# Residual tokens reloaded two at a time into other buffers, and a new order of the mixer's weight rings, in a hybrid decoder layer

## The chip, the core and the metric

The kernel runs on one core of one Trainium2 chip. The metric is device time in microseconds (us), the median of three runs. TensorE (PE) does the matmuls and transposes, VectorE (DVE) and ScalarE (ACT) evacuate and split, GpSimd (POOL) does a few small operations, and SyncE (SP) issues almost all DMAs, in one queue in program order.

## What is computed

One layer on 512 tokens of width 1024, all in float32:

```python
def hybrid_layer(x, ...):
    h = rms_norm(x, ffn1_pre_g)
    x = x + 0.5 * rms_norm(swiglu(h, ffn1_w_gate, ffn1_w_up, ffn1_w_down), ffn1_post_g)
    h = rms_norm(x, mix_pre_g)
    q, k, v, z, xbc, dt = jnp.split(h @ w_in, IN_SPLITS, axis=-1)
    attn = diff_attention(q, k, v, lam, attn_subln_g, lambda_init)
    ssm = ssd_mixer(z, xbc, dt, conv_w, conv_b, dt_bias, a_log, d_skip, ssm_norm_g)
    x = x + rms_norm(jnp.concatenate([attn, ssm], axis=-1) @ w_out, mix_post_g)
    h = rms_norm(x, ffn2_pre_g)
    x = x + 0.5 * rms_norm(swiglu(h, ffn2_w_gate, ffn2_w_up, ffn2_w_down), ffn2_post_g)
    return x
```

The feed-forward width is 2816; the mixer has 8 attention heads with two softmax maps each and 16 state-space heads in 2 groups, scanned in 4 chunks of 128 tokens.

## The kernel before

**Stages.** The program has three stages, f1 (first feed-forward), mix (the mixer) and f2 (second feed-forward). Each opens a pool of on-chip buffers of its own over the same memory, so a buffer of one stage has to wait for those of the stage before that lay on its addresses, buffer by buffer. `places` sets the order of the buffers in a stage, and so which ones lie over which.

**Rings.** `s.t` hands out buffers by tag. Each tag is a ring of a fixed number of buffers, and a new tile waits until the last reader of the tile that held its buffer is through. In f1 and f2: `w` (15 buffers of 4 KB in each partition: split weights, and through `k4` also gains, squares and normed tokens), `hid`, `raw` (3 buffers of 8 KB: weights as they come from memory), `S`, `cv`, `T`. In mix: `kc` (2 of 4 KB), `blk` (6 of 8 KB), `ka`, `kb` (3 of 4 KB), `raw`, `whi`, `wlo` (4 of 4 KB each).

**Products.** A float32 operand is split into a high part (ACT cast, L238 or L333) and a low part (DVE subtraction, L239 or L334), and a product is three matmuls, high by high, high by low and low by high (`mm3`, L254 to L258). A weight therefore goes DMA, `raw`, ACT, DVE, PE.

**The end of a stage.** `halves` forms the last product in two column halves. In the second one, for each of four tiles of 128 tokens (t = 0 to 3), DVE adds PE's result to the accumulator (L534), ACT sums squares (L535), and `finish` follows: `postnorm` (DVE L545, POOL L199 and L200, DVE L547 and L549, the last adding the residual token), the store of x (POOL), and `prenorm_T` (ACT L206, POOL, DVE L215, PE transposes L220, ACT and DVE L224 into `hb`). `finish` of f1 and f2 takes the residual token from `reload`, one load of one tile into a buffer of `w` (L1100); `finish` of the mixer loads it into a buffer of `kc` (L1065).

**The start of f2.** SP loads the gain `pre2`, a raw block of the gate weights, one of the up weights and one of the down weights (L247, L484). Each of the first two holds two units (`pairwise`). The splits of these four units come first on DVE (four times L239), POOL adds high and low parts of `hb` (L286, two instructions), and PE begins with the first unit (L438), eight matmuls high by high before the low part is asked for. Unit 1 of the loop (`load_unit`, L340) needs the next raw gate block.

**The state-space part.** Per chunk, `decay` has POOL build two operands (L854), PE multiply them (L866), ACT take the exponential (L867) and DVE multiply by a mask (L869). `chunk` has PE transpose (L878), DVE scale (L880), PE multiply into the one buffer of `po` (L886), DVE read it (L902 or L905) and ACT sum squares (L206, followed by L199 and L200 on POOL). The input convolutions (DVE L638 and L641) and the projections of the other group run beside it.

**What sets the order.** The order of the instructions on each engine is made when the program is built, by a scheduler that works on its own estimate of times and places; it is fixed when the program runs. Waits on buffers enter that estimate, so a change in buffers can move instructions far away from it.

Of the kernel before, what the change touches and what calls it, by code (L numbers as in the profile page):

```python
# [11 lines left out]
F32 = mybir.dt.float32  # L12
# [5 lines left out]
P = 128  # L18
D = 1024
S = 512  # L20
NT = S // P
KT = D // P
# [7 lines left out]
class Layer:  # L30
# [22 lines left out]
    def places(s):  # L53


        if s.ffn_stage:
            s.t([P, 16], F32, "place", 1, s.stage)
            s.w([P, KT, P])
            s.t([P, 2, S], F32R, "hid", 6, s.stage)
            s.raw([P, KT, 256])  # L60
            s.t([P, 16], F32, "place_S", 1, s.stage)
            s.t([P, 4, S], F32R, "S", 3, s.stage)
            s.m(tag="cv")
            s.t([P, KT, P], F32, "T", 2, s.stage)
            return
        s.m(tag="dd")
        s.k4([P, D], tag="kc")
        s.blk([P, 4, S])
        s.k4([P, D], tag="ka")
        s.k4([P, D], tag="kb")  # L70
        s.k4([P, D], tag="bc")
        s.t([P, S], F32, "state", 1, s.stage)
        for tag in ("cbm", "bn"):
            s.sm(P, 1, tag)
        s.sm(P, 1, "u1r", F32R)
        s.m(tag="cv")
        n = 64
        s.sm(n, 1, "dt"), s.sm(n, 1, "a"), s.sm(n, 1, "ah", F32R), s.sm(n, 1, "al", F32R), s.sm(3 * n, 1, "dec")
        s.sm(8, 8, "s1"), s.sm(4, 4, "mx"), s.sm(4, 4, "se"), s.sm(2, 4, "c2"), s.sm(8, 2, "ms8"), s.sm(8, 2, "ee8")
        for tag in ("whi", "wlo"):  # L80
            s.t([P, KT, P], F32R, tag, 4, s.stage)
        s.raw([P, KT, P])

    def blk(s, shape, dt=F32):
        return s.t(shape, dt, "blk", 6, s.stage)
# [873 lines left out]
def mix(fg, bg, ratio):  # L959

    due = 0.0
    for _ in fg:
        due += ratio
        while due >= 1.0:
            next(bg, None)
            due -= 1.0


def mixer(s, w_in, w_out, x1_d, x2_d, gain, nx):
    nc = s.nc  # L970
    s.qk, s.xs, s.bc, s.z = {}, {}, {}, {}
    qu = lambda j, part: s.proj_T(w_in, (Q0, K0)[part] + j * P, s.evac_q(j, part))
    run = lambda g: [None for _ in g]
    s.dist = s.m(tag="dd")
    nc.gpsimd.iota(s.dist, pattern=[[1, S]], base=-384, channel_multiplier=-1, allow_small_or_imprecise_dtypes=True)
    nc.gpsimd.affine_select(s.dist, s.dist, pattern=[[-1, S]], base=384, channel_multiplier=1,
                            compare_op=ALU.is_ge, fill=NEG)
    run(s.units([s.proj_N(w_in, V0, s.evac_v())] + [qu(0, i) for i in range(2)]))
    s.o = s.blk([P, 4, S])
    units = dict(d=s.dt_unit(w_in), z=s.proj_N(w_in, Z0, s.evac_z(0)), y=s.proj_N(w_in, Z0 + S, s.evac_z(1)))  # L980
    for j in range(1, 4):
        units[f"q{j}"], units[f"k{j}"] = qu(j, 0), qu(j, 1)
    for g in range(2):
        for i, u in enumerate(s.xbc_units(w_in, g)):
            units[f"{'xw'[g]}{i}"] = u

    def operand(src, col0, step):
        hi, lo = (s.blk([P, 4, S], F32R) for _ in range(2))
        for i in range(4):
            c = col0 + step * i  # L990
            s.to_T(lambda t: src(t, i), s.cols[:, c:c + 1], hi[:, i, :], lo[:, i, :])
        return hi, lo

    def attention_out():
        s.acc = [s.ac([P, 2, D]) for _ in range(2)]
        op = operand(lambda t, i: s.o[:, i, t * P:(t + 1) * P], 60, 0)
        wt = s.load_out(w_out, 0)
        yield
        for t in range(NT):
            s.out_tile(wt, *op, t)  # L1000
            yield

    p1 = attention_out()
    op2 = []

    def stream(names):


        names = names.split()
        i = 0  # L1010
        while i < len(names):
            j = i
            while j < len(names) and names[j] in units:
                j += 1
            if j > i:
                yield from s.units([units[n] for n in names[i:j]])
                i = j
                continue
            if names[i] == "P":
                next(p1)  # L1020
            else:
                op2.extend(operand(lambda t, i: s.z[0][:, t, i * P:(i + 1) * P], 61, 1))
            yield
            i += 1

    bg = stream("k1 d q1 q3 z q2 k2 k3 x4 y x1 x3 x5 x0 x2")
    s.lag = 5

    def need(j):
        while (j, 1) not in s.qk:  # L1030
            next(bg)

    due = 0.0
    for j in s.attention(2, need):
        due += [1.38, 1.17, 0.94, 1.07][j]
        while due >= 1.0:
            next(bg, None)
            due -= 1.0
    run(bg)
    bg = stream("w0 w3 w1 w2 w4 w5 P")  # L1040
    mix(s.ssd(0), bg, 0.91)
    run(bg)
    bg = stream("P P P O P")
    mix(s.ssd(1), bg, 0.28)
    run(bg)
    s.lag = 0
    hi, lo = (s.blk([P, 4, S], F32R) for _ in range(2))

    def op3(t):
        ts = slice(t * P, (t + 1) * P)  # L1050
        ps = s.pt()
        for i in range(4):
            nc.tensor.transpose(ps[:, i * P:(i + 1) * P], s.z[1][:, t, i * P:(i + 1) * P], s.ident)
        for i in range(4):
            col = s.cols[:, 65 + i:66 + i]
            pi = ps[:, i * P:(i + 1) * P]
            nc.scalar.activation(hi[:, i, ts], pi, AF.Copy, scale=col)
            nc.vector.scalar_tensor_tensor(lo[:, i, ts], pi, col, hi[:, i, ts].bitcast(F32),
                                           op0=ALU.mult, op1=ALU.subtract)

    def finish(t, at, ss):
        if t == 0:
            s.h = s.new_h()
        xr = s.k4([P, D], tag="kc")
        nc.sync.dma_start(xr, x1_d[t * P:(t + 1) * P, :])  # L1065
        s.postnorm(at, ss, nx["post"], xr, at, False)
        nc.gpsimd.dma_start(x2_d[t * P:(t + 1) * P, :], at)
        if t < 2:
            return s.prenorm_T(at, t, nx["pre"], s.h)

    s.halves(s.acc, lambda c: s.load_half(w_out, S, 4, slice(c * S, (c + 1) * S)),
             lambda k: [(op2 if k < 4 else (hi, lo))[i][:, k % 4, :] for i in range(2)], 4,
             ((s.pa, s.pa, s.pa, s.po), (s.pb, s.pb, s.pa, s.pa)),
             gain, finish, op3)


def layer(tc, x_d, ffn1_pre_g, ffn1_w_gate, ffn1_w_up, ffn1_w_down, ffn1_post_g, mix_pre_g, w_in,
          lq1, lk1, lq2, lk2, subln, conv_w, conv_b, dt_bias, a_log, d_skip, norm_g, w_out, mix_post_g,
          ffn2_pre_g, ffn2_w_gate, ffn2_w_up, ffn2_w_down, ffn2_post_g, out):
    nc = tc.nc  # L1080
    with tc.tile_pool(name="sb", bufs=1) as pool, tc.tile_pool(name="ps", bufs=8, space=PSUM) as psum, \
            tc.tile_pool(name="dr", bufs=1, space=bass.MemoryType.DRAM) as dram:
        s = Layer(tc, pool, psum, dram)
        s.consts()
        x1_d = dram.tile([S, D], F32, name="x1_d")
        x2_d = dram.tile([S, D], F32, name="x2_d")
        nx = {}

        def gain(key, row, pre=None):
# [5 lines left out]
                return nx[key]  # L1095
            return f

        def reload(src, t):
            xr = s.w([P, D], F32)
            nc.sync.dma_start(xr, src[t * P:(t + 1) * P, :])  # L1100
            return xr


        with s.in_stage("f1"):
            x = [s.w([P, D], F32) for _ in range(NT)]

            def load_x(t):
                nc.sync.dma_start(x[t], x_d[t * P:(t + 1) * P, :])

            load_x(0)  # L1110
            g = s.bcast(ffn1_pre_g)
            load_x(1)
            h = s.new_h()
            for t in range(2):
                s.prenorm_T(x[t], t, g, h, (s.pt, s.pb)[t], True)

            def rest1(more):
                for t in range(2, NT):
                    ins = s.prenorm_T(x[t], t, g, h, (s.pt, s.pb)[t % 2], more=more(t))
                return ins  # L1120

            def finish1(t, at, ss):
                if t == 0:
                    s.h = s.new_h()
                s.postnorm(at, ss, nx["post1"], reload(x_d, t), at, True)
                nc.gpsimd.dma_start(x1_d[t * P:(t + 1) * P, :], at)
                return s.prenorm_T(at, t, nx["pre"], s.h)

            s.ffn(h, ffn1_w_gate, ffn1_w_up, ffn1_w_down, gain("post1", ffn1_post_g, mix_pre_g), finish1, rest1,
                  [lambda: load_x(2), lambda: load_x(3)], [1, 2, 3],  # L1130
                  lambda: s.mixer_consts(conv_w, conv_b, dt_bias, a_log, d_skip, subln, norm_g, lq1, lk1, lq2, lk2))
        with s.in_stage("mix"):
            mixer(s, w_in, w_out, x1_d, x2_d, gain("post", mix_post_g, ffn2_pre_g), nx)
# [50 lines left out]
```

## Time and profile before

| what | value |
|---|---|
| median of 3 runs | 1113.23 us (1112.94 to 1117.01) |
| the profiled execution: its own time, its span | 1113.93 us, 1112.2 us |
| PE busy, mean granted clock | 94% of the span, 0.982 |
| DVE, ACT, POOL busy | 71%, 46%, 9% |
| share of 16 DMA engines | 33% (queue of SP), 1% (queue of POOL) |
| stages by PE's first matmul | f1 from 0, mix from 387.45 us, f2 from 748.48 us |

PE is the engine that is busy nearly all the time, so what counts is where it is not. Its idle time and the low granted clock lie at the two changes of stage and in the state-space part; the rows on these places stand below.

### The profile page before, as it was taken

What the parts mean: (1) busy time and instruction counts of PE and PEld (TensorE: products, weight loads), DVE (VectorE), ACT (ScalarE), POOL (GpSimd) and SP (SyncE); (2) the same over time, 40 slices, a digit from 0 to 9 for tenths busy, and PEclk for the clock granted to TensorE, in tenths of its full rate; (3) what the DMA queues carried; (4) which work ended last, traced back from release to release, by engine and by line L of the source; (5) the groups of instructions that cost most, each with busy time, mean ns of one, the idle gap of its engine ahead of it and who ended that gap; (6) DMA issues with size and microseconds to landing.
All of it is one profiled execution on the core that took longest, in us unless ns stands there. A gap on an engine that the chain in (4) does not pass through costs nothing. (4 is left out here: it accounts for less than half of the span.)

```text
span 1112.2 us, 16467 instructions
## 1 busy us (share of the span) xinstructions
PE 1048.1 (94%) x6571; PEld 930.8 (84%) x6571; DVE 786.0 (71%) x1190; ACT 511.6 (46%) x863; POOL 102.2 (9%) x136
## 2 busy tenths in 40 slices
PE   6899999999999599999999999969999999999996
PEld 6899898998998487888887777859898989989985
DVE  6977777756856724675888978658777678667745
ACT  5564443533543423465654345426653435434531
POOL 5001000000000400000022342041000000000001
PEclk9999999999999799999999989989999999999999
DMA  8233232332323453553341102064242323323231
GB/s 272 88 115 115 77 114 77 115 114 75 97 95 98 170 145 97 147 147 91 95 114 48 47 19 90 25 213 147 77 148 70 124 77 114 114 76 113 77 133 76
DMA packets 93996, 118.08 MB, mean 106 GB/s; under 512 B 5436, under 2 KB 73056, under 8 KB 93920
## 3 DMA queue, kind: packets, MB, share of 16 engines
q1 hardware_dynamic: 92384, 112.80, 33.4%
q0 software_dynamic: 1536, 4.23, 1.0%
q8 instruction: 51, 0.84, 0.3%
q14 instruction: 25, 0.20, 0.1%
HBM read 104.43 MB, written 6.29 MB: 100 GB/s over the span
## 5 line engine op out<-in xcount | busy, mean ns | idle before, releaser
L369 PE MATMUL pa<-hb,w 128*128 128x256 f32 x960 | 127.2, 281 | 5.3 <-DVE w L334 5.1
L369 PE MATMUL pt<-hb,w 128*128 128x256 f32 x960 | 128.0, 279 | 2.5 <-DVE w L334 2.5
L369 PEld LDWEIGHTS pa<-hb,w 128*128 128x128 f32 x960 | 119.8, 188 | 9.7 <-DVE w L334 7.5
L369 PE MATMUL pa<-S,w 128*128 128x256 f32 x960 | 123.1, 279 | 0.8 <-ACT cv L399 0.8
L334 DVE TENSOR_TENSOR w<-raw,w 128x1024 fp32r<-128x1024 f32 x80 | 97.8, 1223 | 36.2 <-PE pt L369 14.8
L369 PEld LDWEIGHTS pt<-hb,w 128*128 128x128 f32 x960 | 119.4, 188 | 3.4 <-DVE w L334 2.9
L369 PEld LDWEIGHTS pa<-S,w 128*128 128x128 f32 x960 | 117.4, 188 | 3.1 <-ACT cv L399 2.6
L239 DVE TENSOR_TENSOR w<-raw,w 128x1024 fp32r<-128x1024 f32 x52 | 68.2, 1322 | 55.8 <-PE pa L369 27.2
L333 ACT CAST w<-raw 128x1024 fp32r<-128x1024 f32 x80 | 84.2, 1053 | 40.9 <-PE pc L496 13.5
L238 ACT CAST w<-raw 128x1024 fp32r<-128x1024 f32 x52 | 54.2, 1051 | 99.2 <-PE pa L369 47.7
L496 PE MATMUL pb<-w,hid 128*128 128x512 f32 x384 | 95.6, 392 | 2.3 <-ACT hid L412 2.3
L496 PEld LDWEIGHTS pb<-w,hid 128*128 128x128 f32 x384 | 69.8, 188 | 15.8 <-ACT hid L412 2.7
L239 DVE TENSOR_TENSOR wlo<-raw,whi 128x1024 fp32r<-128x1024 f32 x44 | 55.2, 1268 | 36.7 <-ACT whi L238 36.6
L199 POOL TENSOR_SCALAR r<-ss 128x1 f32<-128x1 f32 x32 | 16.1, 505 | 681.8 <-DVE ss L545 624.8
L496 PE MATMUL po<-w,hid 128*128 128x512 f32 x192 | 74.5, 390 | 0.0
L496 PE MATMUL pc<-w,hid 128*128 128x512 f32 x192 | 74.5, 390 | 0.0
L340 DVE TENSOR_TENSOR T<-raw 128x1024 f32<-128x1024 f32 x40 | 48.9, 1223 | 27.7 <-DMA raw<-in_ffn_w_up_dram 17.1
L238 ACT CAST whi<-raw 128x1024 fp32r<-128x1024 f32 x44 | 45.5, 1049 | 40.1 <-PE pc L257 18.2
L369 PE MATMUL pt<-S,w 128*128 128x256 f32 x480 | 61.8, 280 | 1.4 <-DVE S L309 0.8
L369 PEld LDWEIGHTS pt<-S,w 128*128 128x128 f32 x480 | 58.9, 188 | 2.4 <-DVE S L309 1.0
L348 ACT CAST w<-raw 128x512 fp32r<-128x512 f32 x40 | 25.0, 624 | 73.5 <-PE pt L369 30.4
L333 ACT CAST w<-T 128x1024 fp32r<-128x1024 f32 x40 | 42.0, 1051 | 31.0 <-PE pt L369 23.1
(347 smaller groups left out, 2232.8 us busy)
## 6 DMA issues: line engine op xcount, KB each, us to landing
raw<-in_ffn_w_gate_dram SPq DMA_DIRECT2D x21, 1024.0 KB, 5.5
raw<-in_ffn_w_up_dram SPq DMA_DIRECT2D x21, 1024.0 KB, 5.4
raw<-in_ffn_w_down_dram SPq DMA_DIRECT2D x16, 1024.0 KB, 5.0
raw<-in_w_in_dram SPq DMA_DIRECT2D x32, 512.0 KB, 4.8
raw<-in_ffn_w_down_dram SPq DMA_DIRECT2D x12, 512.0 KB, 3.7
blk<-kc SPq DMA_DIRECT2D x96, 64.0 KB, 2.0
raw<-in_w_out_dram SPq DMA_DIRECT2D x12, 512.0 KB, 3.6
w<-in_x_dram SPq DMA_DIRECT2D x8, 512.0 KB, 4.0
```

The costliest lines, as they stand in the source:

```text
L199: nc.gpsimd.tensor_scalar(r, ss, mul / n, eps, op0=ALU.mult, op1=ALU.add)
L238: s.nc.scalar.copy(hi, raw)
L239: s.nc.vector.tensor_sub(lo, raw, hi)
L333: nc.scalar.copy(hi, x)
L334: v.tensor_sub(lo, x, hi)
L340: v.tensor_add(T13.rearrange("p (h k) f -> p h k f", h=2), r[:, 0:4, :].rearrange("p k (h f) -> p h k f", h=2), odd.rearrange("p (h k) f - ...
L348: nc.scalar.copy(t4[:, 0], r[:, 4:8, :P])
L369: i = mm(ps[:, cs], x[:, k, :], y[:, k, :], start=first and head is None, stop=k == 3 and x is wl, skip_group_check=True)
L496: nc.tensor.matmul(pd[c], a[:, ts], w[:, c * S:(c + 1) * S], start=st, stop=sp)
```

## The change

`reload` (f1 and f2) takes a pair of token tiles in one buffer of the ring `raw`, for t = 0 and t = 2, with two loads each. `finish` of the mixer takes such a pair in one block of the ring `blk` instead of single buffers of `kc`. In `places`, the mixer's ring `raw` comes before `whi` and `wlo`.

```diff
         s.sm(8, 8, "s1"), s.sm(4, 4, "mx"), s.sm(4, 4, "se"), s.sm(2, 4, "c2"), s.sm(8, 2, "ms8"), s.sm(8, 2, "ee8")
+        s.raw([P, KT, P])
         for tag in ("whi", "wlo"):
             s.t([P, KT, P], F32R, tag, 4, s.stage)
-        s.raw([P, KT, P])
...
     hi, lo = (s.blk([P, 4, S], F32R) for _ in range(2))
+    held = {}
...
         if t == 0:
             s.h = s.new_h()
-        xr = s.k4([P, D], tag="kc")
-        nc.sync.dma_start(xr, x1_d[t * P:(t + 1) * P, :])
-        s.postnorm(at, ss, nx["post"], xr, at, False)
+        if t % 2 == 0:
+            held[0] = s.blk([P, 2, D])
+            for i in range(2):
+                nc.sync.dma_start(held[0][:, i, :], x1_d[(t + i) * P:(t + i + 1) * P, :])
+        s.postnorm(at, ss, nx["post"], held[0][:, t % 2, :], at, False)
...
+        held = {}
+
         def reload(src, t):
-            xr = s.w([P, D], F32)
-            nc.sync.dma_start(xr, src[t * P:(t + 1) * P, :])
-            return xr
+
+            if t % 2 == 0:
+                held[0] = s.raw([P, 2, D])
+                for i in range(2):
+                    nc.sync.dma_start(held[0][:, i, :], src[(t + i) * P:(t + i + 1) * P, :])
+            return held[0][:, t % 2, :]
```

By the addresses of the built program, the mixer's four buffers of `raw` lay over f1's `S`, `cv` and `T` and now lie over f1's third buffer of `raw` (the first of them also over the last 64 bytes of the second) and its first `S`. The two pairs of x in f1 go into the second and the first buffer of f1's `raw`. The gain `pre2` of f2 lies, before and now, over the mixer's `dd` and the beginning of the first `kc`; f2's raw up block lay over the mixer's `whi` and now lies over its `raw`.

The SP queue from the mixer's last loads of w_out to f2's first weights (`x_d` is the mixer's saved residual; a number is that of a tile), before:

```order
L1065 DMA kc_6850<-x_d 128x1024
L943 DMA raw_6747<-in_w_out_dram 128x2x512
L943 DMA raw_6753<-in_w_out_dram 128x2x512
L1065 DMA kc_6909<-x_d 128x1024
L1065 DMA kc_6946<-x_d 128x1024
L192 DMA w_6967<-in_ffn_pre_g_dram 128x1024
L247 DMA raw_6971<-in_ffn_w_gate_dram 128x8x256
L247 DMA raw_6973<-in_ffn_w_up_dram 128x8x256
```

And now:

```order
L943 DMA raw_6745<-in_w_out_dram 128x2x512
L943 DMA raw_6751<-in_w_out_dram 128x2x512
L1068 DMA blk_6789<-x_d 128x1024 x2
L1068 DMA blk_6906<-x_d 128x1024 x2
L192 DMA w_6963<-in_ffn_pre_g_dram 128x1024
L247 DMA raw_6967<-in_ffn_w_gate_dram 128x8x256
L247 DMA raw_6969<-in_ffn_w_up_dram 128x8x256
```

The four reloads now stand behind all loads of w_out and write into two blocks.

DVE in `finish` of f1 (L549 takes the residual of a tile, L215 its norm; the tiles 0 and 1 are in `ac_141`, 2 and 3 in `ac_142`), before:

```order
L215 SCALAR_TENSOR_TENSOR w_3630<-ac_141,r_3627,w_3455 128x1024
L534 TENSOR_TENSOR ac_142<-ac_142,pb_3699 128x512
L549 SCALAR_TENSOR_TENSOR ac_141<-ac_141,r_3671,w_3668 128x1024
L224 TENSOR_TENSOR hb_3612<-pt_3632,hb_3611 128x4x128
L545 TENSOR_TENSOR ss_485_3459<-ss_485_3459 128x1
L547 TENSOR_TENSOR ac_142<-ac_142,w_3453 128x512
L224 TENSOR_TENSOR hb_3614<-pt_3639,hb_3613 128x4x128
L215 SCALAR_TENSOR_TENSOR w_3683<-ac_141,r_3680,w_3455 128x1024
```

And now:

```order
L215 SCALAR_TENSOR_TENSOR w_3631<-ac_141,r_3628,w_3455 128x1024
L549 SCALAR_TENSOR_TENSOR ac_141<-ac_141,r_3670,raw_3615 128x1024
L534 TENSOR_TENSOR ac_142<-ac_142,pb_3698 128x512
L224 TENSOR_TENSOR hb_3612<-pt_3633,hb_3611 128x4x128
L224 TENSOR_TENSOR hb_3614<-pt_3640,hb_3613 128x4x128
L215 SCALAR_TENSOR_TENSOR w_3682<-ac_141,r_3679,w_3455 128x1024
L545 TENSOR_TENSOR ss_485_3459<-ss_485_3459 128x1
L547 TENSOR_TENSOR ac_142<-ac_142,w_3453 128x512
```

The residual of tile 1 now comes ahead of tile 2's evacuation, and the norm of tile 1 ahead of tile 2's sum; on ACT the square of tile 1 (L206) has likewise passed that of tile 2 (L535).

POOL where the second group of the state-space part begins (L199 and L200 follow the last chunk of the first group, L854 prepares the decays of the second), before:

```order
L854 TENSOR_TENSOR kb_6188<-u_174_1146,ah_4256 128x1024
L854 TENSOR_TENSOR kb_6190<-u_174_1146,al_4257 128x1024
L854 TENSOR_TENSOR kb_6269<-u_174_1146,ah_4256 128x1024
L199 TENSOR_SCALAR r_6076<-ss_6074 128x1
L200 TENSOR_TENSOR r_6076<-r_6076,mhalf_68 128x1
L854 TENSOR_TENSOR kb_6271<-u_174_1146,al_4257 128x1024
```

And now:

```order
L854 TENSOR_TENSOR kb_6186<-u_174_1146,ah_4254 128x1024
L854 TENSOR_TENSOR kb_6188<-u_174_1146,al_4255 128x1024
L199 TENSOR_SCALAR r_6074<-ss_6072 128x1
L200 TENSOR_TENSOR r_6074<-r_6074,mhalf_68 128x1
L854 TENSOR_TENSOR kb_6267<-u_174_1146,ah_4254 128x1024
L854 TENSOR_TENSOR kb_6269<-u_174_1146,al_4255 128x1024
```

The norm's two small instructions now come ahead of the third decay's operand. Around this place, from the fourth pair of attention heads to the end of the state-space part, PE, DVE and ACT carry the same instructions as before in a somewhat different order; outside of the places named here their orders are the same, but for a neighbour or two.

## Rows read from the trace of the kernel before

**Rows 1.** Timelines of four engines at f2's start: start, length, what, count, [idle before, its releaser]

```profile
740.62 0.63 ACT L535 ACTIVATE m<-ac 128x512 f32<-128x512 f32 x1 [2.95 <-DVE ac L534]
747.38 1.04 ACT L238 CAST w<-raw 128x1024 fp32r<-128x1024 f32 x1 [6.03 <-DMA raw<-in_ffn_w_gate_dram]
...
742.87 1.28 DVE L549 SCALAR_TENSOR_TENSOR ac<-ac,r,kc 128x1024 f32<-128x1024 f32 x1 [0.73 <-POOL r L200]
748.46 2.38 DVE L239 TENSOR_TENSOR w<-raw,w 128x1024 fp32r<-128x1024 f32 x1 [4.30 <-ACT w L238]
752.56 3.50 DVE L239 TENSOR_TENSOR w<-raw,w 128x1024 fp32r<-128x1024 f32 x3 [1.73 <-ACT w L238]
760.50 1.23 DVE L340 TENSOR_TENSOR T<-raw 128x1024 f32<-128x1024 f32 x1 [0.42 <-DMA raw<-in_ffn_w_gate_dram]
...
745.09 4.66 POOL L286 TENSOR_TENSOR hid<-hb,hb 128x1024 f32<-128x1024 f32 x2
...
748.48 2.08 PE L438 MATMUL pa<-hb,w 128*128 128x256 f32 x8 [8.68 <-ACT w L238]
768.12 1.45 PE L369 MATMUL pt<-hb,w 128*128 128x256 f32 x10 [1.56 <-DVE w L334]
```

**Rows 2.** Window before f2: PE, PEld, DVE, ACT, POOL busy, clock, DMA, GB/s

```profile
740.00:745.00 5.00, 0.00 (x0) 0.00 (x0) 2.58 (x4) 0.72 (x2) 1.66 (x3) 0.72 0.99 278
```

**Rows 3.** Timeline of SP's queue there, columns as in Rows 1

```profile
724.95 6.45 SPq L1065 DMA_DIRECT2D kc<-x_d  x2
...
738.19 0.39 SPq L247 DMA_DIRECT2D raw<-in_ffn_w_gate_dram  x1
739.87 0.38 SPq L247 DMA_DIRECT2D raw<-in_ffn_w_up_dram  x1
...
754.95 0.37 SPq L328 DMA_DIRECT2D raw<-in_ffn_w_gate_dram  x1
```

**Rows 4.** Timelines of DVE, ACT, SP and PE from f1 to the mixer

```profile
365.73 1.28 DVE L549 SCALAR_TENSOR_TENSOR ac<-ac,r,w 128x1024 f32<-128x1024 f32 x1
369.72 1.28 DVE L215 SCALAR_TENSOR_TENSOR w<-ac,r,w 128x1024 f32<-128x1024 f32 x1 [0.84 <-POOL r L200]
...
367.46 1.07 ACT L206 ACTIVATE w<-ac 128x1024 f32<-128x1024 f32 x1
...
366.69 1.98 SPq L579 DMA_DIRECT2D raw<-in_w_in_dram  x4
...
387.45 1.22 PE L256 MATMUL pa<-whi,hb 128*128 128x512 f32 x2 [1.62 <-ACT whi L238]
```

**Rows 5.** Timelines of PE, DVE and POOL in the state-space part

```profile
599.68 2.00 PE L886 MATMUL po<-kc,kb 128*128 128x64 f32 x16 [1.15 <-DVE kc L880]
...
635.76 3.12 PE L886 MATMUL po<-kc,kb 128*128 128x64 f32 x16 [2.63 <-DVE m L902]
...
654.15 2.00 PE L886 MATMUL po<-kc,kb 128*128 128x64 f32 x16 [2.58 <-DVE kc L880]
...
634.28 0.74 DVE L638 SCALAR_TENSOR_TENSOR cv<-pa,cols,cv 128x509 f32<-128x509 f32 x1
...
650.90 2.60 DVE L869 TENSOR_TENSOR kb<-kb,cbm 128x1024 f32<-128x1024 f32 x1
...
650.51 1.91 POOL L854 TENSOR_TENSOR kb<-u,ah 128x1024 fp32r<-128x1024 f32 x1 [2.26 <-PE pb L866]
```

**Rows 6.** Windows of 1 us after the wait at 635.76, columns as in Rows 2

```profile
636.00:637.00 1.00, 1.00 (x9) 1.00 (x8) 1.00 (x3) 1.00 (x2) 0.00 (x0) 0.67 0.03 8
...
643.00:644.00 1.00, 1.00 (x7) 0.88 (x6) 0.00 (x0) 0.25 (x1) 0.00 (x0) 0.91 0.00 0
```

**Rows 7.** Timelines of PE and DVE some 30 us earlier: readers of the buffers concerned

```profile
705.47 1.03 PE L1053 MATMUL pt<-ident,blk 128*128 128x128 f32 x8
716.51 1.23 DVE L239 TENSOR_TENSOR wlo<-raw,whi 128x1024 fp32r<-128x1024 f32 x1
```

**Rows 8.** Chain of work that ended last: start, length, what

```profile
739.87 11.59 DMA raw<-in_ffn_w_up_dram
```

## The prediction

> **What bounds the kernel now.** I read the busy shares first, then the waits of PE, then the timelines of the engines around each wait. PE is busy 94% of the span, so the time is PE's work, at the clock that it is granted, plus PE's waits. The diff touches two changes of stage, and the order of the built program also moves in the state-space part; these three places are the terms of the sum.
>
> The largest wait is the start of f2. PE stands still for 8.68 us before its first matmul at 748.48 [rows 1], and its clock has fallen by then, to a mean of 0.72 of full speed in 740 to 745 us [rows 2]. ACT's cast at 747.38 waited for the raw gate weights [rows 1], which SP asked for only at 738.19, the up weights only at 739.87 [rows 3]. The reason stands ahead of them in the queue: the reloads of tiles 2 and 3 at 724.95 each wait for a buffer of `kc` that the residual of an earlier tile must have left, and the gain behind them lies over `kc` too. So SP, which has nothing to do there, holds back weights whose buffers are free or nearly so.
>
> At the change from f1 to mix SP sends the mixer's first weights at 366.69, and PE uses them at 387.45 [rows 4]: no load is late there. What PE waits for is the chain of the four tiles' norms. In the state-space part PE waits 1.15, 2.63 and 2.58 us for DVE ahead of L886 [rows 5]. After the second of these the clock falls to half at about 636.35 (0.67 of full speed over 636 to 637) and is back at about 643.2 (0.91 over 643 to 644) [rows 6]: 6.9 us at the lower of its two levels, 1.2 GHz, where PE does half of the work, a loss of up to 3.4 us.
>
> **The change part by part. Start of f2.** With the reloads in `blk`, none of them waits for another reload. The second block is free when PE's transposes L1053 are through, at 706.5 [rows 7]. The gain and the gate block behind it have free buffers, and the up block waits for the last split of w_out, at 717.74 [rows 7]. So everything is asked for by about 718.5. In the trace the up block took 11.6 us [rows 8], with two other blocks and the gain in flight; even so the last would land before 732, and the first use is at 741. The load of both is hidden. What it would cost if it were not: at most the 6.0 us that ACT waits now [rows 1].
>
> What is late next is ACT's square of tile 3, 740.62 plus 0.63 and 0.1 for reading the sum. The first cast then ends at 742.35 instead of 748.42, and PE starts its first eight matmuls 6.1 us earlier. They ask for no low part; the next ones do, and DVE makes it behind the residual of tile 3, which ends at 744.15 [rows 1]. So the first low part is ready at 744.2 + 1.15 = 745.35 instead of 750.84: 5.5 us earlier.
>
> Here the gain shrinks. The first split took 2.38 us, the three behind it 3.50 together, 1.17 each [rows 1]: the first one ran into POOL's two additions, which end at 749.75, and finished 1.1 us after them. Now all four splits meet these additions, which begin at 745.09 behind their own wait for tile 3. If POOL and DVE take turns, with 2.33 us for an addition, the second split ends at 748.85, the third at 752.35 and the fourth at 753.5; if POOL runs both in a row, they end at 750.9, 752.1 and 753.2. The third was at 754.9, and with it the next gate block is asked for (754.95 [rows 3]). Its transfer took 5.5 us, until DVE's L340 at 760.50 [rows 1]. So L340 starts at 757.9, and all that hangs on DVE from there is 2.6 us earlier.
>
> The Trainium skill's page "SBUF — State Buffer", section "SBUF: two separate sides", says that a DVE operation with two SBUF inputs and a GpSimd operation that reads SBUF lock each other out for the whole instruction, and the loser fully blocks. The trace agrees (2.38 against 1.17 us). It speaks against asking for weights so early: without the lock the third split would end at 747.7, and the term would be bounded by PE's own 4.7 us instead of 2.6.
>
> PE itself is 4.7 us earlier at the third unit (it waits for the third split at 752.35, where it stood at 756.9), so it runs dry sooner, and waits at the place of 768.12 for about 2.5 us instead of 1.56 [rows 1]. After 1.56 us the clock stayed up; after 2.63 it fell for 6.9 us [rows 5, 6]. If it falls here, PE loses 1.7 (half as long) to 3.4 us of the 2.6. Bounds of this term: 4.7 earlier, where the loads of PE and DVE hide each other better than I think, and 0.8 later. I take 1.5 earlier, between 2.6 and nothing, since the wait is nearest in length to those after which the clock fell.
>
> **End of f1.** The loads of x come early and block nothing. SP's first weights for mix now wait for the residual of tile 1 (365.73 plus 1.28 [rows 4]), about as late as now; they have 18 us. What moves is the order: L549 of tile 1 no longer stands behind tile 2's evacuation, though it waits for POOL until 365.5, so it gains 0.2 us. Its square on ACT no longer waits behind tile 2's (366.9 instead of 367.46 [rows 4]), but the norm L215 now stands behind the second L224, and comes at 369.35 instead of 369.72: 0.4 us. Tile 2 gains about 0.9, and tile 3 loses part of it, since its sum now stands behind the norm of tile 2. I come to 0.5 us less until PE's start at 387.45, between 0 and 1.3.
>
> **State-space part.** Nothing is added or removed; the order differs. DVE is what PE waits for in all three places [rows 5], so I count what stands on DVE ahead of the instruction that releases PE. Ahead of the first L880 there is one split fewer, about 1.2 us as in [rows 1], and PE has 14 bulk matmuls more between transposes and L886: the first wait all but goes. Ahead of L902 of the chunk that PE waits for at 635.76 there is one L638 fewer, 0.74 us [rows 5], with PE's work ahead of it unchanged: PE arrives 1.2 us earlier, is released 0.74 earlier, and so waits longer. Net 0.7 us until there. At 654.15 DVE's L869 took 2.60 us, against 1.2 free, because POOL's L854 had begun at 650.51 [rows 5]; now POOL does the norm's two small instructions first, and L869 can go ahead: 1.4 us, less one L862 of 0.3 that now stands ahead of L880. With a shorter wait the clock may stay up, for which I add 0.7. Sum 0.7 + 1.1 + 0.7 = 2.5 us earlier. Behind 660 us PE is busy throughout, so it is kept. The ends are wide, since each move of an L854 can put 1 to 1.5 us on a DVE instruction: 6 us earlier (all three waits and one fall of the clock gone) to 6 us later (one more wait of 2.6 with 3.4 behind it).
>
> **End of f2.** The reloads come earlier and write to `raw`; DVE's chain to the outputs is the same. Nothing.
>
> **Sum.** 1.5 + 0.5 + 2.5 = 4.5 us, from 1113.93 (span 1112.2 and 1.7 around it) to 1109.4. The median of the runs is 0.7 below the profiled execution, so the forecast is 1113.23 - 4.5 = 1108.7 us, 0.4% faster. About 0.5%, 5.6 us, is what a measurement of this kernel can tell from no change.
>
> **The rivals. A, the earlier weights pay in full:** the clock stays up at f2's start and one of the falls in the state-space part goes: 2.6 + 0.5 + 2.5 and 3 more, 8.6 us, 1104.6. For it: PE's later start of that wait can be covered by the second halves of the lead products. Against: DVE is as busy as PE there.
> **B, it is given back:** PE loses 3.4 us to the clock in f2 where DVE gave 2.6, and the waits in the state-space part move without shrinking: about 1 us, 1112.2. For it: the wait of 2.5 us estimated at f2's start. The Trainium skill's page "TensorE: Matmul & The Clock Gate", section "HAM oscillation", describes this: a wait for data lets the clock fall, and each restart pays again. By it the term of f2 is nothing; the trace shows it after 2.63 us and not after 1.56.
> **C, slower:** `po` has one buffer, so L886 of a chunk waits until DVE has read the chunk before. Where the new order leaves DVE later than PE by more than about 2.6 us at two more chunks, each costs 2.6 and up to 3.4 by the clock, 12 in all, less the 4.5 of the sum: 1120.7. For it: DVE's saturation. Against: DVE has less ahead at two of the chunks, not more.
> **D, the change does not do what it says:** SP is held by another buffer, say by the last split of w_out moving late or a block held by the second product, and f2's weights still come behind 735: f2 gives nothing, 3 us remain, 1110.2. Against: the readers at 706.5 and 717.74 [rows 7] leave 20 us.
>
> **How the numbers follow.** Forecast 0.48 (2 to 7 us less), A 0.19, B 0.20, C 0.07, D 0.06. Faster by over 0.5% (below 1107.7) are A and some 0.19 of the forecast: 0.38. Slower by over 0.5% is C: 0.07. The rest is 0.55. The range reaches from 1103.5 into the middle of A to 1114.0 past B; what is outside is C, the far part of A, and little else.
>
> **What would show it.** Right if SP asks for f2's gate and up blocks before 720, PE starts f2 some 3 us after its last matmul of mix, and DVE's first four splits run beside L286. The clock behind the wait at the place of 768 decides between forecast, A and B; L886 in the second and third chunk decides C. Wrong if the cast of the gate weights still waits for a DMA, or if the state-space part moves by more than 6 us either way.

## The result, and the profile after

The changed kernel takes 1102.92 us (median of 4 runs, 1101.16 to 1104.84) against 1114.62 us for the kernel before, whose runs now number four as well: a ratio of 0.9894, 95% interval 0.9865 to 0.9922, or 11.7 us. The forecast was 1108.7 in a range of 1103.5 to 1114.0. So the sign was right, and the gain was more than twice what was forecast and outside the range. The profiled execution has a span of 1100.1 us, 12.1 less than that of before.

Laying the two traces side by side at instructions that both have shows where the 12.1 us come from. At the last evacuations of the mixer (L534) the changed kernel is 10.9 us ahead, so nearly all of the gain lies in f1 and the mixer: 9.35 in the window below, 0.8 at f1's end, 0.3 in the attention, and 0.4 that had come in f1 before its end. Behind f2's first units it is 12.4 ahead, so the start of f2 gave 1.5.

**The state-space part.** Two windows, one in each kernel, begin and end at the same instructions: from a matmul of the fourth pair of attention heads to an evacuation at the end of the mixer. First before, then after; the columns are those of [rows 2], with the window's length first.

```profile
533.92:711.96 178.04, 170.30 (x855) 137.95 (x855) 146.61 (x241) 91.65 (x180) 45.23 (x34) 0.97 0.23 69
```

```profile
532.39:701.08 168.69, 165.76 (x855) 134.27 (x855) 143.13 (x241) 92.21 (x180) 45.03 (x34) 1.00 0.27 81
```

The window is 9.35 us shorter. PE's idle time (length less busy time) falls from 7.74 to 2.93 us, 4.81 less. The same 855 matmuls take 165.76 us instead of 170.30, 4.54 less, because the clock stays at full speed (1.00 against 0.97). The two add up to the whole. PE's timeline in the changed kernel at the places of [rows 5], with the idle time before an instruction and its releaser in brackets:

```profile
595.99 1.89 PE L886 MATMUL po<-kc,kb 128*128 128x64 f32 x16
...
629.52 1.97 PE L886 MATMUL po<-kc,kb 128*128 128x64 f32 x16
...
635.00 0.66 PE L833 MATMUL pt<-ident,blk 128*128 128x128 f32 x4 [0.45 <-DVE blk L835]
...
644.92 0.33 PE L893 MATMUL pt<-ident,bc 128*128 128x128 f32 x1 [1.00 <-DVE cbm L862]
645.52 2.00 PE L886 MATMUL po<-kc,kb 128*128 128x64 f32 x16 [0.27 <-DVE kc L880]
```

The waits of 1.15 and 2.63 us are gone, and 2.58 has become 1.00 and 0.27.

**The start of f2.** Timelines of SP, ACT, DVE, POOL and PE in the changed kernel:

```profile
698.72 0.43 SPq L247 DMA_DIRECT2D raw<-in_ffn_w_gate_dram  x1
706.88 0.38 SPq L247 DMA_DIRECT2D raw<-in_ffn_w_up_dram  x1
...
741.17 0.37 SPq L328 DMA_DIRECT2D raw<-in_ffn_w_gate_dram  x1
```

```profile
730.35 1.03 ACT L238 CAST w<-raw 128x1024 fp32r<-128x1024 f32 x1
...
731.97 1.28 DVE L549 SCALAR_TENSOR_TENSOR ac<-ac,r,blk 128x1024 f32<-128x1024 f32 x1 [0.73 <-POOL r L200]
733.17 9.11 DVE L239 TENSOR_TENSOR w<-raw,w 128x1024 fp32r<-128x1024 f32 x4
...
746.64 1.23 DVE L340 TENSOR_TENSOR T<-raw 128x1024 f32<-128x1024 f32 x1 [0.61 <-DMA raw<-in_ffn_w_gate_dram]
...
734.18 5.88 POOL L286 TENSOR_TENSOR hid<-hb,hb 128x1024 f32<-128x1024 f32 x2
...
731.43 2.08 PE L438 MATMUL pa<-hb,w 128*128 128x256 f32 x8 [2.53 <-ACT w L238]
734.44 3.77 PE L438 MATMUL pa<-hb,w 128*128 128x256 f32 x16 [0.93 <-DVE w L239]
...
752.08 0.47 PE L369 MATMUL pt<-hb,w 128*128 128x256 f32 x2 [0.82 <-DVE hid L300]
754.26 1.80 PE L369 MATMUL pt<-hb,w 128*128 128x256 f32 x10 [1.70 <-DVE w L334]
```

The gate and up weights are asked for 32 and 23 us before the first cast, PE's standstill is 2.53 us instead of 8.68, and the four splits of DVE, 4.7 us of work, take 9.11 beside the two additions of POOL. Behind the waits of 0.82 and 1.70 us the clock falls once more (windows of the changed kernel, columns as in [rows 2]):

```profile
731.00:738.00 7.00, 5.64 (x24) 5.34 (x25) 6.27 (x5) 5.10 (x7) 5.27 (x5) 0.52 0.19 76
...
755.00:759.00 4.00, 4.00 (x23) 4.00 (x23) 4.00 (x7) 0.00 (x0) 0.00 (x0) 0.57 0.00 0
```

### The profile page after: what moved, and what is told of

The parts are those of the page before. It is cut to its first block, busy times and chain, and to the rows that moved or that the text cites. A ratio compares the mean times of both kernels' runs of the same rounds, so it can differ in the third digit from the quotient of the medians.

```text
span 1100.1 us, 16461 instructions
## 1 busy us (share of the span) xinstructions
PE 1046.5 (95%) x6571; PEld 930.2 (85%) x6571; DVE 785.3 (71%) x1190; ACT 511.9 (47%) x863; POOL 103.4 (9%) x136
## 5 line engine op out<-in xcount | busy, mean ns | idle before, releaser
L334 DVE TENSOR_TENSOR w<-raw,w 128x1024 fp32r<-128x1024 f32 x80 | 97.7, 1222 | 37.4 <-PE pt L369 14.8
L239 DVE TENSOR_TENSOR w<-raw,w 128x1024 fp32r<-128x1024 f32 x52 | 71.4, 1385 | 49.0 <-PE pa L369 26.4
L199 POOL TENSOR_SCALAR r<-ss 128x1 f32<-128x1 f32 x32 | 15.6, 488 | 682.7 <-DVE ss L545 629.0
L340 DVE TENSOR_TENSOR T<-raw 128x1024 f32<-128x1024 f32 x40 | 48.9, 1222 | 28.7 <-DMA raw<-in_ffn_w_up_dram 18.1
```

The lines of the kernel that those rows point to most:

```text
L199: nc.gpsimd.tensor_scalar(r, ss, mul / n, eps, op0=ALU.mult, op1=ALU.add)
L239: s.nc.vector.tensor_sub(lo, raw, hi)
L334: v.tensor_sub(lo, x, hi)
L340: v.tensor_add(T13.rearrange("p (h k) f -> p h k f", h=2), r[:, 0:4, :].rearrange("p k (h f) -> p h k f", h=2), odd.rearrange("p (h k) f - ...
```

## Experiments

### The parts of the change alone

In the built programs the three parts do quite different things. The pairs of x in f1 and f2 carry the whole new order of f1's end and of the state-space part. The mixer's pairs in `blk` move SP's last loads and nothing else. The new order of the rings moves no instruction at all. So the parts can be run one by one.

`e1_reload` takes the pairs in f1 and f2 alone:

```diff
-            xr = s.w([P, D], F32)
-            nc.sync.dma_start(xr, src[t * P:(t + 1) * P, :])
-            return xr
+            if t % 2 == 0:
+                held[0] = s.raw([P, 2, D])
+                for i in range(2):
+                    nc.sync.dma_start(held[0][:, i, :], src[(t + i) * P:(t + i + 1) * P, :])
+            return held[0][:, t % 2, :]
```

> The kernel before with the pairs of x in the ring raw in f1 and f2 alone; the mixer's finish still loads single tiles into kc, and its rings stand in the old order. In the built program this part alone carries the whole new order of f1's end and of the state-space part. Theory O (the gain of the mixer is the order): the two waits of 2.6 us before L886 and both falls of the clock in the state-space part are gone, the end of f1 is 0.8 us shorter, the start of f2 keeps its 8.7 us of standstill; 10 to 11 us faster than before, ratio 0.990 to 0.991. Theory B (the gain is the buffers and earlier loads of the mixer): no more than the 0.8 us of f1's end, ratio 0.999. Theory V (the waits of before come and go from one execution to the next): some third set of waits.

Measured: 1105.36 us, ratio 0.9918 (0.9895 to 0.9941), 9.1 us, a little under the 10 to 11 that were expected. PE's waits in the state-space part are those of the changed kernel to 0.01 us (0.45, 1.00, 0.26), no clock falls there, and PE's standstill before f2 stays at 8.45 us.

`e2_block` takes the mixer's `finish` alone:

```diff
-        xr = s.k4([P, D], tag="kc")
-        nc.sync.dma_start(xr, x1_d[t * P:(t + 1) * P, :])
-        s.postnorm(at, ss, nx["post"], xr, at, False)
+        if t % 2 == 0:
+            held[0] = s.blk([P, 2, D])
+            for i in range(2):
+                nc.sync.dma_start(held[0][:, i, :], x1_d[(t + i) * P:(t + i + 1) * P, :])
+        s.postnorm(at, ss, nx["post"], held[0][:, t % 2, :], at, False)
```

> The kernel before with the mixer's finish in blk alone. The order on PE, DVE, ACT and POOL is that of before, on SP only the last loads of the mixer move. Theory O: f2's gate weights are asked for before 720 us, PE's standstill before f2 falls from 8.7 to 2.5 us, and after DVE's crowded splits and one fall of the clock 1.5 us are left, ratio 0.9985; the state-space part has its two waits of 2.6 us and both falls of the clock as before. Theory B: the waits of the state-space part shrink here, 5 us or more, ratio 0.995 or less. Theory V: waits other than before's at the same order.

Measured: 1112.87 us, ratio 0.9989 (0.9972 to 1.0007), 1.2 us. The interval holds 1, so the runs alone cannot tell this from no change. In the trace f2's start gives 1.3 us (2.3 ahead of before at the mixer's end, 3.6 at f2's end).

`e3_rings` takes the order of the rings alone:

```diff
+        s.raw([P, KT, P])
         for tag in ("whi", "wlo"):
             s.t([P, KT, P], F32R, tag, 4, s.stage)
-        s.raw([P, KT, P])
```

> The kernel before with the ring raw of the mixer ahead of whi and wlo alone. Not one instruction moves on any engine; only addresses change. Theory O: no change, ratio 1.000, within 0.2%, the same waits at the same places in the trace. Theory B: the mixer's first weights land earlier or later and the state-space part moves by several us. Theory V: with the same order, waits and falls of the clock in the state-space part differ from those of before by more than 1 us.

Measured: 1114.94 us, ratio 1.0007 (0.9991 to 1.0023).

`e4_both` takes the first two together, without the rings.

> Both reloads changed, the rings of the mixer in the old order: all of the change but its third part. The order on every engine is that of the changed kernel. Theory O: the time of the changed kernel, ratio 0.989 to before, the two other parts adding up (10.5 and 1.5 us). Theory B, if the rings' addresses matter: 2 us or more away from that.

Measured: 1103.32 us, ratio 0.9904 (0.9884 to 0.9925), as the changed kernel. Its up weights are asked for only at 730.67 us, since their buffer lies over `whi` as before; with the rings in their new order this is 706.88. DVE waits 1.25 us for the second cast there, but its four splits end 9.1 us behind the start of the first, as in the changed kernel.

So the gain is the first part's, some 9 to 10 us, plus 1 to 1.5 us from the second by the traces, and the third gives nothing that can be measured. Theory O holds. Theory V falls too: where the order is that of before, the three waits come back to 0.01 us. PE in `e2_block` at the three waits, then in `e3_rings` at the last two:

```profile
599.24 2.00 PE L886 MATMUL po<-kc,kb 128*128 128x64 f32 x16 [1.14 <-DVE kc L880]
...
635.32 2.16 PE L886 MATMUL po<-kc,kb 128*128 128x64 f32 x16 [2.62 <-DVE m L902]
...
652.11 2.00 PE L886 MATMUL po<-kc,kb 128*128 128x64 f32 x16 [2.59 <-DVE kc L880]
```

```profile
635.73 2.81 PE L886 MATMUL po<-kc,kb 128*128 128x64 f32 x16 [2.63 <-DVE m L902]
...
654.12 3.68 PE L886 MATMUL po<-kc,kb 128*128 128x64 f32 x16 [2.58 <-DVE kc L880]
```

What does vary is how long the clock stays down after them. Windows over the state-space part of `e2_block` and of `e3_rings`:

```profile
568.00:710.00 142.00, 135.28 (x688) 108.58 (x688) 116.93 (x164) 69.25 (x127) 41.60 (x32) 0.98 0.22 70
```

```profile
568.00:713.00 145.00, 138.27 (x689) 111.47 (x688) 117.06 (x164) 69.24 (x127) 41.34 (x32) 0.95 0.19 58
```

The same 6.7 us of idle time in both, but a mean clock of 0.98 in one and 0.95 in the other, and with it 3 us of busy time.

### The order without the buffers, and its pieces

`e1_reload` changes buffers and order at once. To part them, the kernel before was given a table that pins the order of PE, DVE, ACT and POOL, with all of its buffers and DMAs kept:

```diff
+ORDER = {
+    "PE": (
...
+def pin(tc):
...
+    for eng, order in ORDER.items():
+        made = traced[eng]
+        for a, b in zip(order, order[1:]):
+            tc.add_manual_dep(made[b], made[a].name,
...
         layer(tc, *args)
+        pin(tc)
```

The new order consists of many small permutations, so it can be put in piece by piece. `e5_order` has all of it in the mixer; `e6_first` up to some 607 us, `e7_second` from 619 to 640, `e8_third` from 643 on.

> The kernel before with every buffer and DMA as it was; a table pins PE, DVE, ACT and POOL to the changed kernel's order from the fourth pair of attention heads to the end of the state-space part, and to before's order elsewhere. If the order alone makes the mixer's gain: PE's three waits before L886 (1.15, 2.63, 2.58 us) shrink to under 0.5 in all at that place, with 1.0 before L893, no fall of the clock there, 8 to 10 us faster than before, ratio 0.991 to 0.993. If the pairs of x in f1's raw are needed for it: waits as before, ratio 1.000.

> The same with the new order only as far as the first chunk of the state-space part (about 541 to 607 us), before's order behind it. By the count of DVE's instructions, as in the prediction: the first wait (1.15 us) goes, PE comes earlier to the second and waits longer there, 3.1 to 3.8 us instead of 2.63, the third stays at 2.58; 0 to 1 us faster. By the rival, that DVE also collides less with POOL and stands idle less in this stretch, which a count of instructions doesn't see: the second wait shrinks too, to under 1.5 us, and its fall of the clock may go; 3 to 6 us faster.

> The same with the new order only around the second wait (619 to 640 us). By the count: one L638 fewer ahead of L902, the wait of 2.63 us shrinks by 0.7 to 1.9, the others stay; by the rival one collision of POOL's L854 with a split goes as well (2.31 us instead of 1.2), the wait shrinks by 1.8 to 0.8 us. The clock may stay up after a wait as short as that: 0.7 to 5 us faster.

> The same with the new order only from the third wait on (from 643 us). POOL does the norm's two small instructions ahead of the third decay's operand, and L869 runs beside nothing, 1.2 us instead of 2.60: the wait of 2.58 us before L886 becomes 1.0 to 1.3 us (before L893 and L886 together), and the fall of the clock behind it goes (1.7 to 3.4 us of PE's time at half speed back); 1.3 to 4.7 us faster, ratio 0.996 to 0.999. The first and the second wait stay at 1.15 and 2.63 us.

Measured: 0.9905 (0.9881 to 0.9929) for the whole, 0.9928 (0.9901 to 0.9956) for the first piece, 0.9989 (0.9976 to 1.0002) for the second, 0.9952 (0.9936 to 0.9968) for the third. PE in `e6_first`, `e7_second` and `e8_third`:

```profile
633.77 1.97 PE L886 MATMUL po<-kc,kb 128*128 128x64 f32 x16 [0.53 <-DVE m L902]
...
647.59 2.00 PE L886 MATMUL po<-kc,kb 128*128 128x64 f32 x16 [0.85 <-DVE kc L880]
...
651.73 1.12 PE L909 MATMUL pb<-kc,bn 128*128 128x512 f32 x2 [1.81 <-ACT bn L895]
```

```profile
637.98 2.37 PE L886 MATMUL po<-kc,kb 128*128 128x64 f32 x16 [2.03 <-DVE m L902]
...
654.78 2.17 PE L886 MATMUL po<-kc,kb 128*128 128x64 f32 x16 [2.58 <-DVE kc L880]
```

```profile
636.37 2.83 PE L886 MATMUL po<-kc,kb 128*128 128x64 f32 x16 [2.64 <-DVE m L902]
...
652.82 0.33 PE L893 MATMUL pt<-ident,bc 128*128 128x128 f32 x1 [0.71 <-DVE cbm L862]
```

The order alone makes the mixer's gain. The second piece does what a count of instructions says: one L638 of 0.74 us fewer ahead of L902, and the wait is 0.60 shorter (as a time it can't be told from no change). The third piece does what the prediction said of POOL: 2.58 becomes 0.71 and 0.27. The first piece is where the count fails: it said that the second wait would grow to 3.1 us or more, and it fell to 0.53.

The pieces do not add up: they make 0.7, 0.1 and 0.5%, the whole makes 1.0. One reason is seen in `e6_first`. Its third wait was expected to stay at 2.58 us, since the order there is that of before, and it fell to 0.85, followed by a new wait of 1.81 for ACT. DVE and POOL there:

```profile
645.71 1.22 DVE L869 TENSOR_TENSOR kb<-kb,cbm 128x1024 f32<-128x1024 f32 x1
...
645.76 2.92 POOL L854 TENSOR_TENSOR kb<-u,ah 128x1024 fp32r<-128x1024 f32 x1 [2.71 <-PE pb L866]
```

In the kernel before, L854 began at 650.51 and L869 at 650.90, and L869 took 2.60 us [rows 5]. Here L869 begins 0.05 us ahead of L854 and takes 1.22, and L854 takes 2.92 instead of 1.91. So with one and the same order a shift of 0.4 us decided which of the two was stretched, and what a piece gains depends on what stands ahead of it.

### What the first piece takes away

Costliest groups of DVE between the attention's last rescaling and L902 of the second wait, in the kernel before and in `e6_first` (busy time and mean ns of one behind the bar):

```profile
L239 DVE TENSOR_TENSOR wlo<-raw,whi 128x1024 fp32r<-128x1024 f32 x14 | 19.0, 1363 | 1.1 <-ACT whi L238 1.1
L869 DVE TENSOR_TENSOR kb<-kb,cbm 128x1024 f32<-128x1024 f32 x4 | 7.6, 1911 | 0.4 <-ACT kb L867 0.4
L641 DVE SCALAR_TENSOR_TENSOR blk<-cv,cv 128x512 f32<-128x512 f32 x5 | 6.2, 1244 | 0.7 <-ACT cv L640 0.7
...
L906 DVE TENSOR_TENSOR blk<-blk,dd 128x512 f32<-128x512 f32 x2 | 2.5, 1250 | 0.0
```

```profile
L239 DVE TENSOR_TENSOR wlo<-raw,whi 128x1024 fp32r<-128x1024 f32 x14 | 18.1, 1296 | 0.9 <-ACT whi L238 0.8
L869 DVE TENSOR_TENSOR kb<-kb,cbm 128x1024 f32<-128x1024 f32 x4 | 7.3, 1819 | 0.7 <-ACT kb L867 0.7
...
L641 DVE SCALAR_TENSOR_TENSOR blk<-cv,cv 128x512 f32<-128x512 f32 x5 | 3.4, 688 | 0.2 <-ACT cv L640 0.2
...
L906 DVE TENSOR_TENSOR blk<-blk,dd 128x512 f32<-128x512 f32 x2 | 1.4, 680 | 0.0
```

The instructions are the same ones, but their durations are not. Of those that read two operands from SBUF, each one that begins while one of POOL's L854 is running is stretched: in the kernel before these are seven DVE instructions, longer than the same ones elsewhere by 8.7 us together; in `e6_first` these four groups take 5.2 us less. Others take 2.8 back (1.9 of it in the attention, 0.7 in another form of L641), so that 6.3 us of stretch are left, 2.4 less. DVE reaches L902 2.6 us earlier, while PE reaches L886 only 0.5 earlier, so the wait shrinks by 2.1.

That is a count from traces. To see the cause by itself, `e9_no_decay_ops` pins the whole order of before and takes away only POOL's reading:

```diff
-                nc.gpsimd.tensor_tensor(mv, s.u2.unsqueeze(1).broadcast_to([P, 8, P]),
-                                        a[:, hs].unsqueeze(2).broadcast_to([P, 8, P]), op=ALU.mult)
+                nc.gpsimd.memset(mv.bitcast(F32), 0.0)
```

> The kernel before, its order on every engine pinned by a table, but POOL's L854 writes zeros instead of multiplying two operands: the decays are left out (their operand is nothing), every other instruction is there. If DVE is late because its instructions run into L854 (8.7 us of stretched DVE instructions between 538 and 636 us): no DVE instruction is stretched there, the second wait shrinks from 2.63 to under 0.5 us, the third from 2.58 to under 1.5, the falls of the clock go, 5 to 9 us faster, ratio 0.992 to 0.9955. If it is late by the count and order of its instructions alone: the waits stay, 0 to 1 us faster.

Measured: 1104.87 us, ratio 0.9910 (0.9879 to 0.9941), with the order of before: 10 us, more than the 5 to 9 that were expected. DVE, POOL and PE in `e9_no_decay_ops` (line numbers behind L854 are one lower, so L868 is L869, L885 is L886, L905 is L906):

```profile
L239 DVE TENSOR_TENSOR wlo<-raw,whi 128x1024 fp32r<-128x1024 f32 x14 | 17.0, 1221 | 1.1 <-ACT whi L238 1.0
...
L868 DVE TENSOR_TENSOR kb<-kb,cbm 128x1024 f32<-128x1024 f32 x4 | 4.9, 1219 | 1.2 <-POOL kb L854 1.2
L641 DVE SCALAR_TENSOR_TENSOR blk<-cv,cv 128x512 f32<-128x512 f32 x5 | 3.4, 688 | 0.7 <-ACT cv L640 0.7
...
L905 DVE TENSOR_TENSOR blk<-blk,dd 128x512 f32<-128x512 f32 x2 | 1.4, 687 | 0.0
```

```profile
L854 POOL MEMSET kb<- 128x1024 f32 x10 | 9.4, 954 | 46.2 <-PE pb L865 12.4 <-PE pt L794 12.2 <-DVE mx L768 11.2
```

```profile
647.39 2.00 PE L885 MATMUL po<-kc,kb 128*128 128x64 f32 x16 [0.78 <-DVE kc L879]
```

No DVE instruction is stretched, the second wait is gone, the first is 0.38, the third 0.78, and the clock stays up. So of the 6.36 us that the three waits of the kernel before make together, 5.2 were made by DVE running into POOL. (The memset also takes only half of the time that L854 took. That is not what helped: in this stretch of the kernel before DVE stood idle 0.4 us for the results of L854, and PE not at all. Nor is it the table that pins the order: `e7_second`, pinned in the same way, has 1.15 and 2.58 us before the first and the third L886.) The Trainium skill's page "SBUF — State Buffer", section "SBUF: two separate sides", says that a DVE operation with two SBUF inputs meets the lock only against a GpSimd operation that reads SBUF; the traces agree on both sides of it: beside L854 the convolution's L638, which reads one operand from PSUM, keeps its 0.73 to 0.75 us in all of these kernels, and beside a memset, which reads nothing, nothing is stretched.

### A version that is faster than both

The same collision is left at f2's start, where the four splits take 9.11 us. `e10_sums_on_dve` gives the two additions of `first` to DVE, behind the splits:

```diff
-        s.nc.vector.tensor_sub(lo, raw, hi)
+        s.last = s.nc.vector.tensor_sub(lo, raw, hi).ins
...
-                nc.gpsimd.tensor_tensor(f, h[b][0][:, :, :256].bitcast(F32), h[b][1][:, :, :256].bitcast(F32), op=ALU.add)
+                with s.tc.issue_after(s.last):
+                    v.tensor_tensor(f, h[b][0][:, :, :256].bitcast(F32), h[b][1][:, :, :256].bitcast(F32), op=ALU.add)
```

> The changed kernel with the two additions L286 of f1 and of f2 on DVE behind the splits instead of on POOL beside them. If the additions on POOL are what crowds the splits: the four splits at f2's start take 4.7 us instead of 9.1, the next gate block is asked for 4 us earlier, DVE's L340 starts 2.5 to 4 us earlier although DVE now does the additions itself (2.4 us), PE's wait of 1.70 us behind it shrinks to under 0.7 and the second fall of the clock may go: 1 to 3.5 us at f2 and 0.5 to 2 us at f1's start against the changed kernel, ratio to before 0.985 to 0.988. If DVE is the bound there whatever it does, the 2.4 us eat it: no change against the changed kernel, 0.989.

> The changed kernel once more, beside the others on the same chip: ratio 0.987 to 0.992 to before, the waits in the state-space part (1.0 before L893, 0.45 and 0.27) and at f2's start (2.5, 0.9, 0.8, 1.7 us) as in its first profile to 0.1 us, while the lengths of the falls of the clock may differ.

Measured: 1097.45 us, ratio 0.9847 (0.9820 to 0.9875) to before; the changed kernel beside it 1102.33 us, 0.9887 (0.9861 to 0.9913), with its waits as in its first profile. DVE and SP in `e10_sums_on_dve` (line numbers one higher behind L286):

```profile
732.93 4.69 DVE L239 TENSOR_TENSOR w<-raw,w 128x1024 fp32r<-128x1024 f32 x4
737.53 2.35 DVE L287 TENSOR_TENSOR hid<-hb,hb 128x1024 f32<-128x1024 f32 x2
...
742.73 1.22 DVE L341 TENSOR_TENSOR T<-raw 128x1024 f32<-128x1024 f32 x1
```

```profile
736.51 0.37 SPq L329 DMA_DIRECT2D raw<-in_ffn_w_gate_dram  x1
```

Against the first profile of the changed kernel, which was 0.2 us behind at this place: the splits take 4.69 us instead of 9.11, the next gate block is asked for 4.4 us earlier, and DVE's first subtraction on it starts 3.7 earlier, though DVE now does 2.35 us of additions more. The wait of 1.70 us and the clock's second fall are gone. Five of its six runs lie about 3 us or more below the fastest run of the changed kernel. f2's start gains 5.0 us by the trace, more than the 1 to 3.5 that were expected; f1's start, where the same was expected to give 0.5 to 2, gives nothing (0.3 us later at f1's end).

## Why the prediction was wrong

**The start of f2: right, step by step.** To compare, 10.9 us, by which the mixer's end came earlier, are to be taken off the predicted times. The gate block was to be asked for behind L1053 and the up block at 717.74, now 706.8: it was at 706.88. The first low part was to be ready at 734.45: PE's second group starts at 734.44. The fourth split was to end at 742.3 to 742.6: it ended at 742.28. The next gate block was to be asked for at 741.2 to 741.5 and L340 to start at 747.0: they were at 741.17 and 746.64. PE's later wait was put at 2.5 us and came as 0.82 and 1.70, and the clock fell for 3.4 us, so rival B's mechanism was there, inside the term: L340 came 3.0 us earlier, and 1.5 of it was lost behind that fall. (The Trainium skill's page "TensorE: Matmul & The Clock Gate", section "HAM oscillation", describes a clock that falls again at each wait for data, in a kernel whose waits are longer. The two falls here are of that kind, but behind waits of 2.53 and of 0.82 and 1.70 us, and they did not bring the term to nothing.) The term was 1.5 us and measured 1.5 in the changed kernel and 1.3 in `e2_block`. That it fits to 0.1 us is luck in part: 1.5 was a choice between 2.6 and nothing. (The 4.7 us for PE at the third unit are 4.55 by the times given with them, 756.9 and 752.35; only an outer bound used them.) Rival D, that SP would still be held, did not happen.

**End of f1: right within its range.** DVE's norm of tile 1 and PE's first matmul of mix in the changed kernel:

```profile
368.66 1.28 DVE L215 SCALAR_TENSOR_TENSOR w<-ac,r,w 128x1024 f32<-128x1024 f32 x1
...
385.84 1.22 PE L256 MATMUL pa<-whi,hb 128*128 128x512 f32 x2 [1.62 <-ACT whi L238]
```

The norm comes 0.6 us earlier than in [rows 4], after 0.4 by which this execution was ahead already; PE's first matmul of mix is 1.2 us earlier by the same reckoning, and 0.8 is left once the clock is back. The term was 0.5, with 1.3 as its end. More can't be said: in `e2_block` and `e3_rings`, with the order of before, the norm of tile 3 came 0.6 us later than in the profile of before by the clock's doing alone.

**The state-space part: the term that failed.** It was 2.5 us, with 6 as its far end; it measured 9.35, and `e5_order`, with the order alone, has the same waits and no fall of the clock. That is beyond the 6 us that the prediction named as a sign of being wrong. The far end was also added up wrongly: the three waits are 6.36 us and one fall of the clock is up to 3.4, which makes 9.8 and not 6. With 9.8 in its place the sum would have reached down to 1101.4 us, below the 1102.92 measured. Of its steps:
- The first wait, 1.15 us, was to go, and did, with 0.4 before another matmul beside it.
- The third, 2.58, was to lose 1.1. It lost 1.3 (and 1.6 in `e8_third`, with before's order ahead of it). The reading of [rows 5], that L854 at 650.51 had doubled L869, was right.
- The second, 2.63, was to grow by 0.5: PE 1.2 us earlier, DVE 0.74. It went. The step that failed is "I count what stands on DVE ahead of the instruction that releases PE". The count was right for what it counts (`e7_second`: 0.60 us for one L638 of 0.74). But it took every instruction at its undisturbed duration, while in the same stretch POOL's ten L854 stretch DVE's instructions by 8.7 us, and a new order changes which of them are hit. `e6_first` shows 2.4 us of this kind, `e9_no_decay_ops` all of it. The prediction had used this very collision twice, for f2's splits and for L869 at the third wait, and did not look for it in the 100 us ahead of the second wait. It even wrote that each move of an L854 can put 1 to 1.5 us on a DVE instruction, as a reason for a wide range, where it was the main term.
- The clock was credited with 0.7 us. The trace of before has two falls there, 6.8 us behind the second wait, whose ends are in [rows 6], and 3.4 behind the third, whose ends are in the windows of the kernel before below (columns as in [rows 2]); both went, which is 4.5 us of PE's busy time. The working took one fall for its far end and did not look for a second one behind a wait of nearly the same length.

```profile
656.00:657.00 1.00, 0.87 (x6) 0.64 (x6) 1.00 (x2) 0.27 (x1) 0.76 (x1) 0.91 0.07 16
...
660.00:661.00 1.00, 1.00 (x5) 0.83 (x4) 1.00 (x2) 0.28 (x1) 0.61 (x2) 0.88 0.00 0
```

In sum, the second wait and the clock make up 3.1 and 3.8 us; small new waits (0.45 and two of 0.14 behind the second chunk) take 0.7 back. The rest of the 6.9 us that are missing is the 0.4 beside the first wait and 0.2 at the third.

**The rivals.** A was nearest by its sum (8.6 us) but not by its mechanism: it saw the surplus in f2, and it came from the mixer. Of the state-space part it had "one of the falls" in it; both belonged there. C did not happen at any chunk.

## What to carry to other kernels

A change of buffers that moves instructions through a scheduler is first of all a change of order, and its largest effect may lie far from the buffers: run the order alone with the old buffers, and the buffers alone with the old order, before either is credited. Where an engine is the one waited for, its late time is the sum of the durations that it had there, not of its instructions at their free duration; list every instruction that is longer than its like, and ask whether the new order still lays it beside what stretched it. And a wait on PE that ends in a fall of the clock is worth more than its length (2.63 us of waiting with 6.8 us at half speed behind it cost up to 6.0 here), so look behind each wait of a kind that has shown one.

## What the runs showed of the hardware

- A POOL operation that reads two operands from SBUF and a DVE operation of the same kind hold each other up, the later one waiting: L869, 1.22 us alone, took up to 2.8, L641 (0.69) up to 2.4, the small L777 (0.22) 1.67, and POOL's own L854 (1.90) up to 2.92. A DVE copy with one SBUF operand was hit too (L778 in `e6_first`: 0.63 us instead of 0.17). A memset of the same 128x1024 on POOL takes 0.95 us and stretched nothing. Moving 2.35 us of work from POOL to DVE, the busier engine, made DVE 3.7 us earlier.
- The waits in the state-space part repeat to 0.01 us from one execution to the next as long as the order is the same; the clock's falls do not. Behind the same wait of 2.63 us the clock was at its lower level for 3.4 us in one trace and 6.8 in three others. PE's clock fell behind waits of 2.0 to 2.6 us in all traces that have them, and behind 0.82 and 1.70 us two microseconds apart; it stayed up in `e6_first` behind 0.85 and 1.81 us four microseconds apart. In `e6_first` and `e7_second` it also fell for 3.4 us at 537 us, behind waits of 0.28 and 0.59, behind which it stayed up in the kernel before. Why, no run here tells.
